# Sums of h from f32 blocks kept at the norm, and seven-product pairs in place of the plain gates

## Chip, cores and metric

The kernel runs on one NeuronCore of a Trainium2 chip. The metric is the device time of one execution in microseconds; the median of the runs counts. The engines are TensorE (PE: matmuls and transposes), VectorE (DVE), ScalarE (ACT), GpSimd (POOL) and SyncE (SP), which issues the DMAs.

## The reference

A decoder trunk of two layers over 1024 tokens of width 1024, in float32. What matters here is the first half of a layer:

```python
for l in range(DEPTH):
    h = rmsnorm(x, norm1[l])
    proj = h @ w_in[l]                       # 1024 x 5120
    qa, ka, va, qb, kb, vb, gate_pre = jnp.split(proj, splits, axis=-1)
    o_a = dilated_mixture(...)               # 12 heads in 3 groups, softmax with ALiBi
    o_b = stick_breaking_attention(...)      # 4 heads
    gates = jax.nn.sigmoid(gate_pre + b_gate[l])    # 2 x 1024 columns
    merged = g_a * (o_a @ w_br[l, :OUT_A]) + g_b * (o_b @ w_br[l, OUT_A:])
    x = x + merged @ w_o[l]
    ...                                      # RMSNorm, gated ConvFFN, residual
```

## The kernel before, in words

**Numbers in two parts.** Each float32 operand of a matmul is kept as a high part in the fp32r format and a low part (the rest). `split` (L133 on) makes them: a copy on ScalarE (L139) gives `hi`, a subtraction on VectorE (L146) gives `lo`. One product takes three matmuls: hi x hi, lo x hi, hi x lo.

**Two ways to multiply by h.** h lies transposed in SBUF: `H[n]` has its high and low parts for token half n, eight blocks k of 128 features by 512 tokens. A *plain* product (`product`, L174 on) adds eight blocks, 8 x 3 = 24 matmuls of 512 columns, for 128 columns of weights and one token half. A *pair* (`pair`, L1053 on) takes two such chunks of weights as one 2 x 2 block matrix and h as another (token half by feature half) and multiplies them by a scheme of seven block products in place of eight. `seven` (L979 on) does one of them, 4 x 3 = 12 matmuls, so a pair has 84 matmuls where two plain chunks have 96. Each pair makes its sums of weights (two on GpSimd at L1075 and L1076, two on VectorE), splits seven pieces of weights (`piece`, into buffers of the tags `wh` and `wl`, four each), and adds partial results on VectorE (`u` tiles). A pair's steps before its first product are seven stages of a generator; `READY` is 6 of them.

**The sums of h.** The scheme also needs four combinations of h's blocks, which are the same for every pair: `S[1]` to `S[4]`, each four tiles of 128 x 512 in two parts. With b11 = h(1,0), b12 = h(0,0), b21 = h(1,1), b22 = h(0,1), where h(n,k) is token half n, feature half k: S1 = b12 - b11, S3 = b22 - b12, S2 = b22 - S1, S4 = b21 - S2 (up to the naming of the blocks). A pair's products take, in this order, h(1,0), S1, S2, h(0,1), S3, h(1,1), S4. `block_sums` (L989 on) makes them from the parts of h, each block being hi + lo: `first` takes three instructions on GpSimd for one quarter of S3 and of S1 (L999, L1004, L1005), `second` two on VectorE (L1012, L1013) for S2, `fourth` three on VectorE (L1019 to L1021) for S4; `in_two` splits them.

**The order.** TensorE's instructions run in the order in which the program emits them. The other engines are ordered by a list scheduler that goes by priority, that is by the place of emission, by readiness and by explicit dependences (`add_manual_dep`, NO_SYNC for order alone). A layer begins with the *head* (`head`, L593 on): values, keys and queries of the first two stick-breaking heads as plain products, beside the norm that still makes h (`first` in layer 0, which normalises eight token blocks as x arrives; `norm`, L513, in layer 1). Then `attend` runs the items of attention: 16 rows of stick-breaking (B), 4 near heads (N), 16 far items (T). Between their small matmuls it calls `dense.advance(rate)`, which emits *units* of six dense matmuls, so many per call as the rate says (`RATE`, `RATE_N`, `RATE_T`). `Dense.choose` (L224) says which: while `plain` has gates, these; then `main`: the near pair 2, `EARLY` gate pairs, and the pairs of values, keys and queries that later items need; and then the other gate pairs (`seven`). The side steps of `block_sums` are emitted one at a time by `aside`, in the head and between units.

**The plain gates.** `gate` (L1207 on) makes one chunk of 128 gate columns for both halves by plain products. The first `PLAIN` = 4 of the 16 chunks of a layer go this way, right behind the head, while the sums of h are made; the other 12 are six pairs (`pair_gate`).

**Buffers** are shared by tag: `e8` (six of 8 KB a partition: the head's weights, the parts of S1 to S3), `xa` (four: x, keys and values of the attention, `stay` rows), `ql` (two: values of the head, raw weights `in_a` of a pair), `p4` (four), `wr` (two: raw weights, `u`), `pt` (six small ones). A tile waits until a buffer of its tag is free.

Of the kernel before, what the change touches and what calls it, by code (L numbers as in the profile page):

```python
# [45 lines left out]
RATE_T = 0.6  # L46
PLAIN = 4
EARLY = 3
# [14 lines left out]
def trunk_kernel(ctx, tc, x, norm1, w_in, b_gate, w_br, w_o, norm2, w_up, conv_w, conv_b, w_down, norm_f, out, depth=None, probe=None):  # L63
# [156 lines left out]
    class Dense:  # L220
# [278 lines left out]

    def new_s(t):  # L500
# [12 lines left out]
    def norm(n, gain, tag, then=None, keep=False):  # L513
# [16 lines left out]
        new_h(n)  # L530
        for e in range(KD):
            hf = kept_f32(n, e) if keep else small("hf")
# [13 lines left out]
    def values_part(vt, w, ms):  # L546
        for m in ms:
# [17 lines left out]
            if m % 2:  # L565
                nc.sync.dma_start(sv[0][:, :, 2 * m - 2 : 2 * m + 2, :], f32(vt[m // 2]))
# [26 lines left out]
    def head(l):  # L593
# [18 lines left out]
        for n in range(2):  # L612
            yield from kq_half(0, wk, n)
            yield from kq_half(1, wq, n)
            if n == 0 and not l:
                yield from values_part(vt, wv, range(2, 4))
        if l:
            yield from values_part(vt, wv, range(2, 4))
# [370 lines left out]
    def block_sums(dense):  # L989


        last, rs = {}, {}

        def first(t, a, b, i):
            if i == 0:
                new_s(t)
                rs[t] = quarter("h_sum") if t == 3 else sb.tile([P, 4, HF], F32, tag="ql", bufs=2, name="h_sum")
            r, (ah, al), (bh, bl) = rs[t][:, i, :], a()[i], b()[i]
            one = pool.tensor_tensor(r, f32(al), f32(bl), ALU.subtract)  # L999
            if last:  # L1000
                tc.add_manual_dep(one.ins, last["sum"], NO_SYNC, reason="one sum after the other")
            else:
                tc.add_manual_dep(one.ins, LAST["h"], SYNC, reason="after h")
            pool.tensor_tensor(r, r, f32(ah), ALU.add)  # L1004
            last["sum"] = pool.tensor_tensor(r, r, f32(bh), ALU.subtract).ins.name  # L1005

        def second(i):
            if i == 0:
                new_s(2)
            in_two(1, i)  # L1010
            r, (ah, al) = rs[1][:, i, :], b22()[i]
            dve.tensor_tensor(r, f32(ah), r, ALU.subtract)  # L1012
            dve.tensor_tensor(r, r, f32(al), ALU.add)  # L1013

        def fourth(i):
            if i == 0:
                S[4] = half(0, 0)
            r, (ah, al) = small("h_sum"), b21()[i]
            dve.tensor_tensor(r, f32(ah), f32(S[2][i][0]), ALU.subtract)  # L1019
            dve.tensor_tensor(r, r, f32(S[2][i][1]), ALU.subtract)  # L1020
            dve.tensor_tensor(r, r, f32(al), ALU.add)  # L1021
            split(*S[4][i], r, "waits")

        def in_two(t, i):
            split(*S[t][i], rs[3 if t == 3 else 1][:, i, :], "waits", LAST["head"])

        b11, b12, b21, b22 = (lambda n=n, k=k: half(n, k) for k in range(2) for n in (1, 0))
        todo = []

        def series(after, lag, gap, f, g):  # L1030

            at = {}
            for i in range(4):
                at.setdefault(i * gap, []).append(lambda i=i: f(i))
                at.setdefault(i * gap + lag, []).append(lambda i=i: g(i))
            for k in range(3 * gap + lag + 1):
                todo.append((after, lambda fs=at.get(k, ()): [h() for h in fs]))

        for i in range(4):
            todo.append((set(), lambda i=i: first(3, b22, b12, i)))  # L1040
        for i in range(4):
# [1045 lines left out]
```

## Time and profile before

| | |
|---|---|
| median of 3 runs | 2643.26 us (2642.09 to 2644.81) |
| profiled execution, its own time | 2642.11 us |
| span in the profile, first to last instruction | 2640.1 us |
| matmuls, all forms | 12780 |
| VectorE, ScalarE, GpSimd busy | 2068.6, 1337.7, 734.9 us |
| DMA | 468.25 MB, mean 177 GB/s |

The profile is of one execution. In its rows, L12 is line 12 of the kernel, an operation is written as out<-in by the names of the tiles, with partitions x elements, and x40 is a count. A group's row gives the busy time, the mean duration of one, and the idle time of the engine just before them with what ended it. In a timeline the first number is the start in us from the beginning of the span and the second how long the instruction, or several merged, took; idle time before stands in brackets. An answer on one tile gives the shortest, median and longest duration in ns and the first and last start. A window row gives, for a stretch of time, the busy time and count of PE, weight loads (PEld), DVE, ACT and POOL, the granted clock of TensorE, the share of the DMA engines and GB/s.

Layer 0's head goes up to about 65 us, its plain gates with the first rows of stick-breaking between them from 65.0 to 120 us, and the first pair follows. In layer 1 the head ends at 1370.2 us and the gates at 1424.4 us.

### The profile page before, as it was taken

How to read it: one execution, taken by the hardware profiler on the slowest of the kernel's cores; microseconds unless marked ns; L12 is line 12 of the kernel's file. 1: busy time of each engine (PE TensorE's matmuls, PEld its weight loads, DVE VectorE, ACT ScalarE, POOL GpSimd, SP SyncE). 2: the span in 40 equal slices, each digit the busy share in tenths (PEclk: the TensorE clock that was granted, in tenths of full speed). 3: DMA queues.
4: the chain of work that ended last, by engine and by line, in shares of the span. 5: the costliest groups of instructions: out<-in, count | busy, mean ns of one | idle time of the engine just before them, and what ended most of it. 6: DMA issues, size and time to landing. Idle time of an engine off the chain costs nothing.

```text
span 2640.1 us, 36792 instructions
## 1 busy us (share of the span) xinstructions
PE 2621.5 (99%) x12780; PEld 2192.0 (83%) x12780; DVE 2068.6 (78%) x3094; ACT 1337.7 (51%) x2488; POOL 734.9 (28%) x612
## 2 busy tenths in 40 slices
PE   9999999999999999999999999999999999999999
PEld 8888888888888888888888888888888888888888
DVE  5887766795888898897659787667858888888865
ACT  5555565564545555432435555666645455554225
POOL 5422201132244343321162212101321343334200
PEclk9999999999999999999999999999999999999999
DMA  7343587873244444688442445797632544357863
GB/s 259 114 144 112 159 220 204 220 253 90 81 146 146 164 146 157 234 310 322 155 154 93 145 140 160 198 236 203 219 101 80 168 144 159 136 176 256 330 247 116
DMA packets 400550, 468.25 MB, mean 177 GB/s; under 512 B 24437, under 2 KB 315629, under 8 KB 398573
## 3 DMA queue, kind: packets, MB, share of 16 engines
q1 hardware_dynamic: 400348, 465.90, 54.9%
q8 instruction: 101, 1.65, 0.3%
q14 instruction: 85, 0.69, 0.1%
q10 hardware_dynamic: 16, 0.00, 0.0%
HBM read 303.23 MB, written 162.59 MB: 176 GB/s over the span
## 4 chain that ended last, share of the span: by engine, by line
PE 83%; DVE 9%; issue 3%; DMA 2%; ACT 2%; POOL 1%; SPq 0%; DVEq 0%; POOLq 0%; ACTq 0%
PE u_a L983 5%; PE u_a L985 5%; PE u_a L984 5%; PE d_ps L1715 5%; PE d_ps L1716 5%; PE d_ps L1717 5%; PE i_a L983 4%; PE i_a L985 4%; PE i_a L984 4%; PE u_c L985 3%; PE u_c L983 3%; PE u_c L984 3%; PE o_ps L180 2%; PE o_ps L181 2%; PE o_ps L182 2%
## 5 line engine op out<-in xcount | busy, mean ns | idle before, releaser
L146 DVE TENSOR_TENSOR w_lo<-up_a,w_hi 128x512 fp32r<-128x512 f32 x240 | 236.7, 992 | 20.2 <-ACT w_hi L139 20.2
L139 ACT CAST w_hi<-up_a 128x512 fp32r<-128x512 f32 x240 | 149.4, 623 | 183.9 <-PE u_a L984 45.9
L1723 DVE TENSOR_TENSOR x<-x,d_ps 128x512 f32<-128x512 f32 (+1 forms) x228 | 151.8, 671 | 78.0 <-PE d_ps L1717 76.6
L1454 POOL TENSOR_TENSOR cv<-cv 128x512 f32<-128x512 f32 x88 | 131.8, 1509 | 248.8 <-DVE cv L1449 138.9
L139 ACT CAST w_hi<-in_a 128x512 fp32r<-128x512 f32 x192 | 119.2, 621 | 117.5 <-PE i_c L984 42.7
L146 DVE TENSOR_TENSOR w_lo<-in_a,w_hi 128x512 fp32r<-128x512 f32 x192 | 141.3, 736 | 36.4 <-ACT w_hi L139 27.0
L146 DVE TENSOR_TENSOR g<-cv,g 128x512 fp32r<-128x512 f32 x154 | 151.7, 986 | 5.2 <-ACT g L139 2.8
L1715 PE MATMUL d_ps<-gd_in,w_hi 128*128 128x512 f32 (+1 forms) x340 | 130.3, 383 | 2.3 <-ACT w_hi L139 1.4
L1717 PE MATMUL d_ps<-gd_in,w_lo 128*128 128x512 f32 (+1 forms) x340 | 129.8, 382 | 0.0
L1716 PE MATMUL d_ps<-gd_in,w_hi 128*128 128x512 f32 (+1 forms) x340 | 129.8, 382 | 0.0
L1075 POOL TENSOR_TENSOR u<-in_a 128x512 f32<-128x512 f32 x32 | 45.8, 1431 | 293.2 <-DMA in_a<-in_w_in_dram 110.5
L983 PE MATMUL u_a<-hh,w_hi 128*128 128x512 f32 x320 | 124.7, 390 | 0.4 <-DVE u L1605 0.3
L984 PE MATMUL u_a<-t_lo,w_hi 128*128 128x512 f32 x320 | 124.5, 389 | 0.0
L985 PE MATMUL u_a<-t_hi,w_lo 128*128 128x512 f32 x320 | 124.5, 389 | 0.0
L985 PE MATMUL u_a<-hh,w_lo 128*128 128x512 f32 x320 | 124.5, 389 | 0.0
L983 PE MATMUL u_a<-t_hi,w_hi 128*128 128x512 f32 x320 | 124.5, 389 | 0.0
L984 PE MATMUL u_a<-hl,w_hi 128*128 128x512 f32 x320 | 124.5, 389 | 0.0
L146 DVE TENSOR_TENSOR w_lo<-w_raw,w_hi 128x512 fp32r<-128x512 f32 x96 | 77.5, 809 | 57.6 <-ACT w_hi L139 52.8
L691 POOL TENSOR_SCALAR_AFFINE_SELECT beta<-beta 128x128 f32<-128x128 f32 x64 | 36.6, 571 | 305.2 <-ACT beta L687 305.2
L139 ACT CAST g<-cv 128x512 fp32r<-128x512 f32 x154 | 94.9, 616 | 39.8 <-POOL cv L1454 29.3
L1715 PE MATMUL d_ps<-gd_in,wd 128*128 128x512 f32 (+1 forms) x292 | 113.9, 390 | 0.0
L1717 PE MATMUL d_ps<-gd_in,wd 128*128 128x512 f32 (+1 forms) x292 | 112.8, 386 | 0.0
(395 smaller groups left out, 8638.0 us busy)
## 6 DMA issues: line engine op xcount, KB each, us to landing
gd<-g SPq DMA_DIRECT2D x154, 512.0 KB, 3.1
gd_in<-gd SPq DMA_DIRECT2D x154, 512.0 KB, 6.3
up_a<-in_w_up_dram SPq DMA_DIRECT2D x80, 512.0 KB, 5.6
in_a<-in_w_in_dram SPq DMA_DIRECT2D x64, 512.0 KB, 5.4
wd_raw<-in_w_down_dram SPq DMA_DIRECT2D x22, 1024.0 KB
gin<-gs SPq DMA_DIRECT2D x32, 512.0 KB, 5.1
w_raw<-in_w_o_dram SPq DMA_DIRECT2D x64, 256.0 KB, 2.9
t_kq<-tk SPq DMA_DIRECT2D x32, 384.0 KB, 5.0
```

The lines of the kernel that those rows point to most:

```text
L139: one = act.copy(hi, src)
L146: two = dve.tensor_tensor(lo, src, f32(hi), ALU.subtract)
L180: pe.matmul(o, lh, rh, start=(first and i == 0), stop=False, skip_group_check=share)
L181: pe.matmul(o, lh, rl, start=False, stop=False, skip_group_check=share)
L983: pe.matmul(o, w[0][:, c], rh, start=(first and i == 0), stop=False, skip_group_check=True)
L984: pe.matmul(o, w[0][:, c], rl, start=False, stop=False, skip_group_check=True)
L985: pe.matmul(o, w[1][:, c], rh, start=False, stop=(last and i == 3), skip_group_check=True)
L1454: return lambda: pool.tensor_tensor(dst, a, b, ALU.subtract)
L1715: pe.matmul(o[:, sub], wh[:, c], gh[:, sub], start=(i == 0 and k in (0, 4, 5)), stop=False, skip_group_check=True)
L1716: pe.matmul(o[:, sub], wh[:, c], gl[:, sub], start=False, stop=False, skip_group_check=True)
L1717: pe.matmul(o[:, sub], wl[:, c], gh[:, sub], start=False, stop=(i == m - 1), skip_group_check=True)
L1723: dve.tensor_tensor(x, x, o[:, sub], ALU.add)
```

## The change

1. The norm keeps h in f32. `raw_h` allocates `RAW[n, k]`, four tiles of 128 x 512 for token half n and feature half k, two in `e8` (n = 0) and two in `xa` (n = 1). The norm writes its f32 result there instead of into a small scratch tile before it is split. In layer 0 the first three token blocks are normalised another way, and `again` fills their 384 columns with hi + lo, eight additions on GpSimd.
2. The sums are made from these f32 blocks: `sum3`, `sum1`, `sum2` on VectorE and `sum4` on GpSimd, one instruction for each quarter, some in place. They are emitted as side steps in the head; S1 and S2 are split there too, S3 and S4 in the first units of the first pair (`begin`).
3. `PLAIN` and `gate` go; all 16 gate chunks are eight pairs, five of them early (`EARLY` 3 to 5). The first pair (near pair 2) follows the head at once.
4. `dense.prime(1)` advances the first pair's preparation by a stage, at fixed places of the head: its loads, its sums on GpSimd, and the splits of three pieces. `{"wv"}` holds the first split back until the values' products have freed `wh` and `wl` in layer 0.
5. Dependences for order alone: a pair's loads behind `LAST["sv"]` (the values' store), its first sum and the clearing of the slots behind `again`. The split of S1 and S2 is no longer put behind the head's last evictions.
6. `RATE_T` goes from 0.6 to 0.55.

```diff
-RATE_T = 0.6
-PLAIN = 4
-EARLY = 3
+RATE_T = 0.55
+EARLY = 5
 ...
+        def prime(self, most):
+            if self.nxt is None:
+                self.nxt = self.choose()
+            self.ready(self.nxt, most)
 ...
+    def raw_h(n):
+        for k in range(2):
+            x = quarter("h_raw") if n else big("h_raw").rearrange("p a (b c) -> p (a b) c", c=HF)
+            RAW[n, k] = x
 ...
-            hf = kept_f32(n, e) if keep else small("hf")
+            hf = kept_f32(n, e) if keep else RAW[n, e // 4][:, e % 4, :] if raw else small("hf")
 ...
-                nc.sync.dma_start(sv[0][:, :, 2 * m - 2 : 2 * m + 2, :], f32(vt[m // 2]))
+                LAST["sv"] = nc.sync.dma_start(sv[0][:, :, 2 * m - 2 : 2 * m + 2, :], f32(vt[m // 2])).ins.name
 ...
-            pool.memset(f32(R["slots"][64:128, :, 1, :]), 0.0)
+            one = pool.memset(f32(R["slots"][64:128, :, 1, :]), 0.0)
+            tc.add_manual_dep(one.ins, LAST["again"], NO_SYNC, reason="behind")
 ...
     def block_sums(dense):
 ...
+        b12, b22, b11, b21 = (lambda i, n=n, k=k: RAW[n, k][:, i, :] for n in range(2) for k in range(2))
+        def sum3(i):
 ...
+            one = dve.tensor_tensor(s3[i], b22(i), b12(i), ALU.subtract)
+            tc.add_manual_dep(one.ins, LAST["h"], NO_SYNC, reason="behind h")
+        def sum1(i):
+            dve.tensor_tensor(b12(i), b12(i), b11(i), ALU.subtract)
+        def sum2(i):
+            dve.tensor_tensor(b11(i), b11(i), s3[i], ALU.add)
+        def sum4(i):
+            pool.tensor_tensor(b21(i), b21(i), b11(i), ALU.subtract)
+        def in_two(t, i):
 ...
+            split(*S[t][i], {1: b12, 2: b11, 3: s3.get, 4: b21}[t](i), "waits", LAST["head"] if t > 2 else None)
+        def front(i):
+            sum3(i)
+            sum1(i)
             in_two(1, i)
+            sum2(i)
+        todo = [(set(), lambda i=i: front(i)) for i in range(4)]
+        todo += [(set(), lambda: dense.prime(1)), (set(), lambda: [sum4(i) for i in range(4)])]
+        todo += [({"wv"}, lambda: dense.prime(1))]
+        todo += [(set(), lambda i=i: in_two(2, i)) for i in range(4)]
+        todo += [(set(), lambda: dense.prime(1)) for _ in range(2)]
         def begin():
             for i in range(4):
-                dense.at(1 + 2 * i, lambda i=i: fourth(i))
+                dense.at(1 + i, lambda i=i: in_two(3, i))
+                dense.at(6 + i, lambda i=i: in_two(4, i))
 ...
-        pool.tensor_tensor(u2, a11, a21, ALU.subtract)
+        one = pool.tensor_tensor(u2, a11, a21, ALU.subtract)
+        tc.add_manual_dep(one.ins, LAST["again"], NO_SYNC, reason="behind")
 ...
-        dense.plain = [gate(l, c) for c in range(PLAIN)]
-        gates = [pair_gate(dense, l, e) for e in range(PLAIN // 2, KD)]
+        gates = [pair_gate(dense, l, e) for e in range(KD)]
 ...
-                hf = small("hf").rearrange("p (e t) -> p e t", e=4)
+                hf = RAW[n, h][:, :, c * P : (c + 1) * P]
 ...
+        def again():
+            t = slice(0, 3 * P)
+            for e in range(KD):
+                k = e % 2
+                hi, lo = (f32(y[:, 4 * k + e // 2, t]) for y in H[0])
+                one = pool.tensor_tensor(RAW[0, k][:, e // 2, t], hi, lo, ALU.add)
+                tc.add_manual_dep(one.ins, LAST["h"], NO_SYNC if e else SYNC, reason="after h")
+            LAST["again"] = one.ins.name
```

More of the change, by code (lines that the diff above doesn't have):

```diff
@@ L989, in block_sums @@
     def block_sums(dense):
-        last, rs = {}, {}
-        def first(t, a, b, i):
-            if i == 0:
[L996 to L1005, printed above, removed]
@@ L1024, in in_two @@
[L1024 to L1037, printed above, removed]
@@ L1204, in pair_gate @@
         return pair(dense, l, (OFF_G + e * P, OFF_G + D + e * P), False, put)
-    def gate(l, c):
-        ab, e = c % 2, c // 2
-        cc = ab * KD + e
-        w = weights(w_in[l][:, OFF_G + cc * P : OFF_G + (cc + 1) * P], P)
-        yield
-        for n in range(2):
-            o = bank("ps", "g_ps")
-            yield from product(o, [(w[k], h_part(n, k)) for k in range(KD)])
-            t = small("gt")
-            act.copy(t, o)
-            nc.sync.dma_start(gs[e, n, :, ab, :], t)
-            yield
     def wo_chunk(l, n, e):
```

65 lines of the change are left out of this document (32 added, 33 removed).

## The prediction

> **What bounds the kernel now.** I read the page of the profile first (its totals, its chain, its rows of slices), then the timeline of TensorE around the place of the change, then the windows by stage, and last the answers on the two tiles that the change removes or re-makes, `g_ps` and `h_sum`.
>
> ```profile
> span 2640.1 us, 36792 instructions
> PE 2621.5 (99%) x12780; PEld 2192.0 (83%) x12780; DVE 2068.6 (78%) x3094; ACT 1337.7 (51%) x2488; POOL 734.9 (28%) x612
> PEclk9999999999999999999999999999999999999999
> PE 83%; DVE 9%; issue 3%; DMA 2%; ACT 2%; POOL 1%; SPq 0%; DVEq 0%; POOLq 0%; ACTq 0%
> ```
>
> TensorE is busy 99% of the span at full granted clock, and 83% of the chain that ended last is on it. Busy alone is weak, since neighbouring matmuls overlap in the record, so I take the pace from the starts. Between the first and the second row here lie the 24 matmuls of one product (8 blocks by 3):
>
> ```profile
> 53.40 0.40 PE L180 MATMUL kq_ps<-hh,kq_w 128*128 128x512 f32 x1
> 58.86 0.39 PE L180 MATMUL q_ps<-hh,kq_w 128*128 128x512 f32 x1
> ...
> 65.04 0.50 PE L180 MATMUL g_ps<-hh,w_hi 128*128 128x512 f32 x1
> ...
> 1358.63 0.28 PE L180 MATMUL v_ps<-v_w,hh 128*128 128x256 f32 x1
> ```
>
> (58.86 - 53.40) / 24 = 0.2275 us for a 512-column matmul. That is the price of one on the path; its recorded 0.39 us is not. The third row is where the head of layer 0 ends and the first plain gate begins.
>
> One rule speaks against the full price: the Trainium skill, "Perfetto Trace Analysis", section Identifying the Most-Contended Engine, says that matmul occupancy misjudges how near TensorE is to its limit and that the busy share of weight loads should be taken beside it. Here that share is 83%, and an estimate by that page would let 83% of the removed time come back, 9.1 us of the 10.9 below. The trace doesn't bear it out in this stretch: 24 matmuls start at an even pace.
>
> **What is removed from TensorE.** The plain gates are these three groups:
>
> ```profile
> L180 PE MATMUL g_ps<-hh,w_hi x128: 389/393/498, 65.0 to 1423.7; 128*128 128x512 f32 x128
> L181 PE MATMUL g_ps<-hl,w_hi x128: 387/389/397, 65.4 to 1424.0; 128*128 128x512 f32 x128
> L182 PE MATMUL g_ps<-hh,w_lo x128: 388/389/403, 65.6 to 1424.2; 128*128 128x512 f32 x128
> ```
>
> 3 x 128 = 384 matmuls, 192 in each layer: four chunks, two halves, 24 each. Two chunks as one seven-product pair take 7 x 4 x 3 = 84. Four chunks thus go from 192 to 168, and 24 matmuls leave each layer: 48 x 0.2275 = **10.9 us** gross. The order behind them stays: in units of six matmuls the gates were 32 and the two new pairs are 28, so everything after comes 4 units earlier. `RATE_T` 0.55 for 0.6 takes about the same 4 units out of the far items (16 items, about 5 calls each, 0.05 less per call), so the tail keeps its filling. The gain is cashed in that stage, if TensorE bounds it, which is weighed among the rivals.
>
> **What the gates covered.** Before, the sums of h were made on GpSimd and VectorE under 52 us of plain gates. After, the first pair starts where 65.04 stands. Its seven products are 12 matmuls, 2.7 us, each: the first needs plain h, the second S1 (+2.7 us), the third S2 (+5.5), the fifth S3 (+10.9), the seventh S4 (+16.4). So S1, S2 and three weight pieces must be made in the head. The first two rows here are the last low parts of h in layer 0, of token blocks 6 and 7 of the eight; the others are gate weights that go (4.3 us):
>
> ```profile
> 38.70 0.69 DVE L146 TENSOR_TENSOR hl<-hf,hh 128x512 fp32r<-128x512 f32 x1 [0.17 <-ACT hh L139]
> ...
> 42.49 0.69 DVE L146 TENSOR_TENSOR hl<-hf,hh 128x512 fp32r<-128x512 f32 x1 [0.69 <-ACT hh L139]
> ...
> 52.09 2.44 DVE L146 TENSOR_TENSOR w_lo<-w_raw,w_hi 128x512 fp32r<-128x512 f32 x2 [2.94 <-ACT w_hi L139]
> ...
> 56.61 0.98 DVE L146 TENSOR_TENSOR w_lo<-w_raw,w_hi 128x512 fp32r<-128x512 f32 x1 [1.48 <-ACT w_hi L139]
> 58.41 0.88 DVE L146 TENSOR_TENSOR w_lo<-w_raw,w_hi 128x512 fp32r<-128x512 f32 x1 [0.81 <-ACT w_hi L139]
> ```
>
> The windows show the room: layer 0 from 44 to the end of the head, and layer 1 (1346 to 1370); the second and third rows are the gates' stretch and the first two pairs of before, the last is from the far stage.
>
> ```profile
> 44.00:65.00 21.00, 21.00 (x133) 18.74 (x131) 6.29 (x7) 4.74 (x9) 20.16 (x16) 1.00 0.64 204
> 64.40:117.00 52.60, 51.49 (x249) 42.26 (x249) 43.77 (x60) 28.71 (x55) 26.00 (x25) 1.00 0.37 114
> 117.00:160.00 43.00, 42.22 (x207) 34.26 (x207) 40.68 (x61) 25.99 (x55) 12.11 (x14) 1.00 0.44 137
> 1346.00:1370.00 24.00, 24.00 (x152) 21.82 (x151) 2.76 (x4) 2.37 (x4) 23.00 (x19) 1.00 0.44 140
> 480.00:520.00 40.00, 40.00 (x247) 35.19 (x245) 31.77 (x64) 20.98 (x51) 5.42 (x6) 1.00 0.69 177
> ```
>
> The columns are the length, then busy time of TensorE, weight loads, VectorE, ScalarE and GpSimd. In both heads GpSimd is full and VectorE nearly empty: 6.29 of 21 us and 2.76 of 24. The change turns that around.
>
> **The new work in the heads.** VectorE gets 12 sums (`sum3`, `sum1`, `sum2`, four each), the 8 low parts of S1 and S2, and 4 instructions of the first pair's pieces. The nearest rows:
>
> ```profile
> L146 DVE TENSOR_TENSOR t_lo<-h_sum,t_hi x24: 658/680/1777, 66.2 to 1416.5; 128x512 fp32r<-128x512 f32 x24
> L1004 POOL TENSOR_TENSOR h_sum<-h_sum,hh x16: 1281/1294/1629, 45.6 to 1376.6; 128x512 f32<-128x512 f32 x16
> L1019 DVE TENSOR_TENSOR h_sum<-hh,t_hi x8: 659/678/1777, 120.1 to 1437.3; 128x512 f32<-128x512 f32 x8
> ```
>
> 24 x 0.68 = 16.3 us on VectorE when it is alone. With GpSimd at work one costs up to 1.78: 1.1 more for each meeting, and this timeline shows three in a row at 1.6 each, beside GpSimd instructions of 1.62 instead of 1.29:
>
> ```profile
> 66.21 4.80 DVE L146 TENSOR_TENSOR t_lo<-h_sum,t_hi 128x512 fp32r<-128x512 f32 x3
> ...
> 67.14 1.62 POOL L1004 TENSOR_TENSOR h_sum<-h_sum,hh 128x512 f32<-128x512 f32 x1
> ```
>
> So one meeting per GpSimd instruction. Layer 0 has `again` (8 additions over 384 of 512 columns, 0.97 us each by that share, from 39.4 to 47 or, with meetings, 49: some 4 after 44), the pair's two weight sums and four `sum4`: about 10 meetings, 11 us; layer 1 has 6, 6.6 us. The Trainium skill, "SBUF — State Buffer", section SBUF: two separate sides, has the same as an exclusive lock, held for the whole instruction, with the other side fully blocked. By that rule a meeting costs up to a whole GpSimd instruction, 1.29 us, the two layers' 16 meetings an estimated 20.6 us where the rows give 17.6, and layer 0 ends 1.9 us later. The trace agrees that one of the two waits, with 1.78 against 0.68.
>
> Layer 0: 21 - 6.29 + 4.3 = 19.0 us are free, and S2 may be 5.5 us later: 24.5. Needed: 16.3 to 27.3. That is from 8 us early (nothing to gain: TensorE is full there) to 2.8 late; the rows of meetings are the nearest, so I take **2.0 us** late. Layer 1: 24 - 2.76 + 5.5 = 26.7 free against 16.3 to 22.9: in time; I take **0.3** for w1, which is wanted at once (bounds 0 and 1). ScalarE (8 + 3 casts) has 16 us free and isn't late. The new waits: `u2` and the slots' clearing stand behind `again` on GpSimd, but the slots are read only by the scores, eight units into the first pair, and `u2` first by its fifth product; the pair's two loads stand behind the first values' store on SP, ahead of the second half's k and q stores, and are issued before half of the head is over. Cover gone there would cost one landing, 5.4 us:
>
> ```profile
> in_a<-in_w_in_dram SPq DMA_DIRECT2D x64, 512.0 KB, 5.4
> ```
>
> **VectorE in the first two pairs.** Of the 43.77 us in the gates' stretch these groups go or move (`in_a` rows: the first pair's pieces):
>
> ```profile
> L146 DVE TENSOR_TENSOR t_lo<-h_sum,t_hi 128x512 fp32r<-128x512 f32 x12 | 11.9, 1018 | 0.0
> L146 DVE TENSOR_TENSOR w_lo<-w_raw,w_hi 128x512 fp32r<-128x512 f32 x4 | 5.0, 1258 | 2.2 <-ACT w_hi L139 2.2
> L1012 DVE TENSOR_TENSOR h_sum<-hh,h_sum 128x512 f32<-128x512 f32 x4 | 3.5, 866 | 0.0
> L1013 DVE TENSOR_TENSOR h_sum<-h_sum,hl 128x512 f32<-128x512 f32 x4 | 2.7, 682 | 0.0
> L146 DVE TENSOR_TENSOR w_lo<-in_a,w_hi 128x512 fp32r<-128x512 f32 x2 | 1.3, 674 | 0.0
> L1080 DVE TENSOR_TENSOR in_a<-in_a 128x512 f32<-128x512 f32 x1 | 0.7, 672 | 0.0
> ```
>
> 43.8 - 25.1 = 18.7 us stay. Added: low parts of S3 and S4 (8), two pairs at 7 low parts, 2 weight sums and 3 additions (24, less 4 in the head), 4 for the near pair's k and q, 4 of the third pair: 36 x 0.68 = 24.5. Together 43.2 us in 52.6 - 5.4 = 47.2: 92%. The stretch 117 to 160 shows what such a load costs: VectorE at 95% (40.68 of 43), TensorE idle 0.78. I take **0.8** a layer (bounds 0 and 2). In turn that later stretch loses the 16 instructions of `fourth`, 10.9 us, and with them at most its 0.78; I take **0.3** a layer back.
>
> Sum: -10.9 + 2.0 + 0.3 + 1.6 - 0.6 = -7.6 us. The profiled execution took 2642.1, 1.2 less than the median of the runs, 2643.3, so 2634.5 in its terms and **2635.6 us** as a median. What a measurement here can tell from no change is 0.2%, 5.3 us.
>
> **The rivals.** *The heads run late.* If the meetings cost what they can (2.8 in layer 0), VectorE takes w1 behind S2 (2.7 more in each layer) and the first pairs wait 2 us in each, then -10.9 + 2.8 + 5.4 + 4.0 = +1.3: 2644.6, no difference. For it: `sum1` needs `again`, which ends only about 49. Against: VectorE's emptiness.
>
> *VectorE becomes the bound of the first pairs (slower).* S1 and S2 live in a group of six buffers that the head's weights and the kept blocks fill. If their buffers came free only when the head ends, 12 low parts and pieces would fall behind it: 12 x 0.68 + 6 x 1.1 = 14.8 us, for which 47.2 - 43.2 = 4.0 us are spare. TensorE waits 10.8 in each layer: -10.9 + 21.6 = +10.7, 2654.0 us. It decides from 9.5 us a layer behind the head on (4.0 spare and half of 10.9). Against it: in layer 1 the k and q weights are last read where the row at 1358.63 stands, 11.6 us before the head ends, and each kept block is free once its sum is made.
>
> *The far stage isn't bound by TensorE.* Then four units less of filling bring nothing, and the costs stay: 2.0 + 0.3 + 1.6 - 0.6 = +3.3, 2646.6, no difference either. By the rule from the Trainium skill's "Perfetto Trace Analysis" above, the weight loads' 35.19 of 40 us in that stage would speak for it in part. Against: the last window has TensorE at 40.00 of 40, VectorE at 31.77. That the matmuls don't go at all I rule out: the counts follow from the code.
>
> **How the numbers follow.** Forecast 0.68, heads late 0.12, far stage 0.05, VectorE the bound 0.15. The forecast's own span goes from all costs nil (10.9 and the later stretches' 1.6 gained: 2630.8) to a gain of 5.3 (2638.0); all costs at their bounds (2.8 + 1 + 4, a gain of 3.1) already belong to the late heads. The range 2631 to 2645 takes the late heads in and leaves out the last two, 0.20. Faster 0.68; within 0.2%: 0.12 + 0.05 and nothing else, 0.17; slower 0.15.
>
> **What would show it.** Right: no `g_ps`; 48 matmuls fewer; GpSimd near half empty in the heads, VectorE near full there; the first pair starting at about 64.4 and 1370.2 and lasting, without the attention's work in it, at most 21 us; VectorE over 90% in the two pairs with under 2 us idle on TensorE. Wrong: `i_a` or `i_c` waiting in the first pair for `t_lo` or `w_lo` by 5 us or more in either layer; matmul starts inside the head spread by evictions queued behind sums; waits in the far items that were not there.

## The result, and the profile after

The changed kernel takes 2669.61 us (median of 4 runs, 2669.03 to 2675.12), the kernel before 2643.15 (4 runs beside it). The ratio is 1.0104, 95% interval 1.0087 to 1.0122: 1% slower, where 2635.6 us had been forecast. The profiled execution took 2669.75 us, its span is 2667.6.

The page of the profile after:

```profile
span 2667.6 us, 36682 instructions
PE 2619.4 (98%) x12732; PEld 2190.2 (82%) x12732; DVE 2072.7 (78%) x3110; ACT 1347.4 (51%) x2500; POOL 696.2 (26%) x588
PE 84%; DVE 9%; DMA 3%; ACT 2%; issue 2%; POOL 0%; SPq 0%; DVEq 0%; ACTq 0%; POOLq 0%
```

TensorE has the 48 matmuls fewer (12780 to 12732), and it idles 48.2 us of the span where it idled 18.6 before. The page doesn't say where; the windows by stage do (length, then busy time of TensorE, weight loads, VectorE, ScalarE, GpSimd, then the granted clock):

```profile
44.00:77.20 33.20, 23.93 (x142) 21.05 (x141) 27.25 (x33) 9.61 (x19) 14.71 (x11) 0.85 0.49 162
57.00:67.20 10.20, 3.40 (x8) 2.75 (x9) 10.20 (x14) 4.84 (x9) 3.84 (x3) 0.50 0.21 77
1357.70:1390.70 33.00, 28.66 (x167) 25.17 (x165) 25.80 (x32) 9.44 (x19) 11.12 (x7) 0.95 0.44 140
...
436.00:563.90 127.90, 125.47 (x733) 108.31 (x732) 88.60 (x197) 74.67 (x168) 14.26 (x15) 0.99 0.81 216
1750.80:1877.90 127.10, 124.35 (x733) 106.91 (x732) 87.91 (x197) 74.46 (x168) 15.08 (x15) 1.00 0.79 217
```

At the end of layer 0's head TensorE now works 24 of 33 us, for 142 matmuls where 21 us held 133 before, and for ten of these microseconds the granted clock is 0.50. The rows of TensorE with their waits, in the two heads and where the first pairs start:

```profile
63.80 0.80 PE L179 MATMUL kq_ps<-hh,kq_w 128*128 128x512 f32 x1 [9.27 <-DVE vb L577]
64.40 0.63 PE L180 MATMUL kq_ps<-hl,kq_w 128*128 128x512 f32 x1
64.82 0.63 PE L181 MATMUL kq_ps<-hh,kq_w 128*128 128x512 f32 x1
...
77.17 0.50 PE L999 MATMUL i_a<-hh,w_hi 128*128 128x512 f32 x1
...
1371.50 0.80 PE L179 MATMUL q_ps<-hh,kq_w 128*128 128x512 f32 x1 [4.34 <-DVE kq_l L593]
```

The first pair starts at 77.17; before, the first gate started at 65.04. TensorE stood 9.27 us, and behind it the matmuls start 0.42 us apart (64.40 to 64.82) instead of 0.2275. It waited for `vb`, the eviction of a values product. This is VectorE's queue in that time, with one row of GpSimd put first:

```profile
53.44 1.61 POOL L1026 TENSOR_TENSOR h_raw<-h_raw 128x512 f32<-128x512 f32 x1 [0.69 <-issue]
...
47.19 2.10 DVE L1016 TENSOR_TENSOR h_sum<-h_raw 128x512 f32<-128x512 f32 x2
49.22 2.38 DVE L1020 TENSOR_TENSOR h_raw<-h_raw 128x512 f32<-128x512 f32 x2
51.52 1.78 DVE L1023 TENSOR_TENSOR h_raw<-h_raw,h_sum 128x512 f32<-128x512 f32 x1
53.23 2.36 DVE L145 TENSOR_TENSOR t_lo<-h_raw,t_hi 128x512 fp32r<-128x512 f32 x2
...
60.19 2.36 DVE L145 TENSOR_TENSOR t_lo<-h_raw,t_hi 128x512 fp32r<-128x512 f32 x2
62.47 0.68 DVE L1023 TENSOR_TENSOR h_raw<-h_raw,h_sum 128x512 f32<-128x512 f32 x1
63.07 1.27 DVE L577 TENSOR_TENSOR vb<-v_ps,vb 128x512 fp32r<-128x512 f32 x2
```

`vb` runs at 63.07, twice in a row. A *bank* is one of the two buffers of the tag `ps` in which products collect. Both had been full, the older one since about 48.6 us (the end of its product), and VectorE had twelve sums and four low parts in its queue ahead, from 47.19 on without a gap: 16 instructions in 15.9 us. Most take 1.0 to 1.8 us instead of 0.68, beside work of GpSimd (E2 below takes that away).

Layer 1's head has a shorter form of it; the row of GpSimd comes first, then ScalarE, then VectorE:

```profile
1365.09 1.73 POOL L1080 TENSOR_TENSOR in_a<-in_a 128x512 f32<-128x512 f32 x1
...
1366.86 0.62 ACT L138 CAST w_hi<-in_a 128x512 fp32r<-128x512 f32 x1 [6.48 <-POOL in_a L1080]
1367.38 0.59 ACT L592 ACTIVATE kq_h<-q_ps 128x512 fp32r<-128x512 f32 x1
...
1369.57 1.28 DVE L1023 TENSOR_TENSOR h_raw<-h_raw,h_sum 128x512 f32<-128x512 f32 x2
1370.77 0.68 DVE L593 SCALAR_TENSOR_TENSOR kq_l<-q_ps,kq_h 128x512 fp32r<-128x512 f32 x1
```

ScalarE idles 6.48 us over a weight cast that waits for GpSimd's weight sum, with the cast of q queued behind; then q's low part stands behind sums on VectorE, and TensorE waits the 4.34 us above for it.

The stages, by the starts of TensorE's matmuls (first pair, or first plain gate before the change; first `z<-t_kq`; first `br_ps`; first `v_ps` of layer 1), lengths in us, of the kernels that the argument uses most; the rest ends with the start of the last matmul, and E numbers are the experiments below:

| | head 0 ends | attention 0 / 1 | far stage 0 / 1 | head 1 | rest, both layers |
|---|---|---|---|---|---|
| before | 65.04 | 356.39 / 354.25 | 128.59 / 128.59 | 46.85 | 1554.7 |
| after | 77.17 | 358.86 / 360.02 | 127.87 / 127.17 | 52.91 | 1557.5 |
| E1 evictions first | 71.56 | 357.54 / 360.85 | 127.90 / 130.54 | 51.81 | 1558.3 |
| E2 no GpSimd in heads | 71.34 | 357.25 / 363.34 | 125.25 / 128.16 | 47.13 | 1556.9 |
| E5 both | 65.61 | 358.08 / 360.21 | 125.52 / 131.68 | 46.85 | 1556.4 |
| E12 pair sums moved | 66.12 | 355.13 / 356.52 | 128.92 / 127.23 | 46.85 | 1557.6 |
| E14 rates shifted | 65.84 | 352.85 / 351.65 | 126.31 / 128.04 | 46.85 | 1556.0 |

After against before: heads +12.1 and +6.1, attention up to the far stage +2.5 and +5.8, far stage -0.7 and -1.4 where -5.5 each were forecast, rest +2.8, all of it in layer 1: +27.1, the difference of the spans within 0.4.

The second place, in the attention. GpSimd's row, then VectorE's, then TensorE's:

```profile
252.19 1.77 POOL L1078 TENSOR_TENSOR u<-in_a 128x512 f32<-128x512 f32 x1 [5.89 <-PE v_t L1175]
254.04 1.29 POOL L1080 TENSOR_TENSOR in_a<-in_a 128x512 f32<-128x512 f32 x1
255.28 0.29 POOL L707 TENSOR_SCALAR_AFFINE_SELECT beta<-beta 128x128 f32<-128x128 f32 x1
...
255.86 1.23 DVE L720 TENSOR_TENSOR_SCAN stay<-stay,zero 128x512 f32<-128x512 f32 x1 [3.05 <-POOL stay L707]
258.32 0.68 DVE L1181 TENSOR_TENSOR vv<-v_t,vv 128x512 fp32r<-128x512 f32 x1
...
259.15 0.55 PE L745 MATMUL sb_o<-sbh,kv 128*128 128x256 f32 x1 [2.93 <-DVE vv L1181]
```

The next pair's weight sums sit on GpSimd ahead of a mask; VectorE's scan waits 3.05 us for the mask, an eviction stands behind the scan, TensorE 2.93 us behind that. These instructions are those of before. The pairs now come four steps of dense work earlier against the items, which is the likely reason that they meet otherwise; no run shows that alone.

### The profile page after: what moved, and what is told of

Read it like the earlier page. It is cut to its first block, busy times and chain, and to the rows that moved or that the text cites. A ratio compares the mean times of both kernels' runs of the same rounds, so it can differ in the third digit from the quotient of the medians.

```text
span 2667.6 us, 36682 instructions
## 1 busy us (share of the span) xinstructions
PE 2619.4 (98%) x12732; PEld 2190.2 (82%) x12732; DVE 2072.7 (78%) x3110; ACT 1347.4 (51%) x2500; POOL 696.2 (26%) x588
## 4 chain that ended last, share of the span: by engine, by line
PE 84%; DVE 9%; DMA 3%; ACT 2%; issue 2%; POOL 0%; SPq 0%; DVEq 0%; ACTq 0%; POOLq 0%
PE u_a L999 5%; PE u_a L1000 5%; PE u_a L1001 5%; PE d_ps L1708 5%; PE d_ps L1710 4%; PE d_ps L1709 4%; PE i_a L999 4%; PE i_a L1001 4%; PE i_a L1000 4%; PE u_c L999 3%; PE u_c L1000 3%; PE u_c L1001 3%; PE o_ps L181 2%; PE o_ps L179 2%; PE o_ps L180 2%; PE i_c L999 2%
## 5 line engine op out<-in xcount | busy, mean ns | idle before, releaser
L138 ACT CAST w_hi<-in_a 128x512 fp32r<-128x512 f32 x216 | 134.1, 621 | 185.3 <-PE i_a L1000 71.3
L145 DVE TENSOR_TENSOR w_lo<-in_a,w_hi 128x512 fp32r<-128x512 f32 x216 | 161.4, 748 | 51.7 <-ACT w_hi L138 43.7
L1078 POOL TENSOR_TENSOR u<-in_a 128x512 f32<-128x512 f32 x36 | 52.6, 1460 | 399.9 <-DMA in_a<-in_w_in_dram 118.0
L720 DVE TENSOR_TENSOR_SCAN stay<-stay,zero 128x512 f32<-128x512 f32 (+2 forms) x96 | 97.2, 1020 | 33.2 <-POOL stay L707 33.0
L999 PE MATMUL i_a<-t_hi,w_hi 128*128 128x512 f32 x288 | 119.9, 416 | 0.0
L999 PE MATMUL i_a<-hh,w_hi 128*128 128x512 f32 x288 | 119.2, 414 | 0.0
L1001 PE MATMUL i_a<-t_hi,w_lo 128*128 128x512 f32 x288 | 114.5, 398 | 0.0
```

What stands on the lines that cost most here:

```text
L138: one = act.copy(hi, src)
L145: two = dve.tensor_tensor(lo, src, f32(hi), ALU.subtract)
L720: one = dve.tensor_tensor_scan(rev, rev, zero[:, 0:1].to_broadcast([P, c1 - c0]), 1.0 if c1 == L else sv[:, c1 : c1 + 1], ALU.mult, ALU.add)
L999: pe.matmul(o, w[0][:, c], rh, start=(first and i == 0), stop=False, skip_group_check=True)
L1001: pe.matmul(o, w[1][:, c], rh, start=False, stop=(last and i == 3), skip_group_check=True)
```

## The experiments

The theory after the result: in the heads, the sums stand ahead of the evictions in the in-order queues, so the two banks fill and TensorE stops (order). The rival: VectorE, slowed by meetings with GpSimd, has too much to do in the head in any order (load). For the attention: masks behind the pairs' sums on GpSimd.

**E1, evictions first.**

```diff
-            one = act.copy(vv[:, :, :, 0:64], ov)
-            two = dve.tensor_tensor(vv[:, :, :, 64:128], ...)
+            with tc.high_priority(offset=AHEAD):
+                one = act.copy(vv[:, :, :, 0:64], ov)
+                two = dve.tensor_tensor(vv[:, :, :, 64:128], ...)
...
-        LAST["head"] = in_parts(c, SCALE, hi, lo, o)
+        with tc.high_priority(offset=AHEAD):
+            LAST["head"] = in_parts(c, SCALE, hi, lo, o)
```

> The changed kernel with the evictions of the head (values, k, q) given priority over the sums on VectorE and ScalarE; the same work on every engine. Order theory (the evictions stand behind the sums in the queues, TensorE finds both banks full): the wait of 9.4 us at 54 us falls to 2 to 5 us, and the half clock behind it goes with it, so layer 0's first pair starts near 70 instead of 77.2 us, layer 1 gains about 3 more, and the time is 2655 to 2662 us. Load theory (VectorE, slowed by its meetings with GpSimd, cannot do the head's work in time whatever its order): the wait only moves behind the head, into the first products of the first pair, which then wait for t_lo, and the time stays at 2666 to 2672 us.

Measured: 2666.66 us (one execution, as in all experiments for which no interval is given; so the lengths of the stages tell more than the time). The time is on the load theory's side, the place on the other: the head of layer 0 ends 5.6 us earlier, and nothing reappears in the first pair. Rows of VectorE, then TensorE:

```profile
51.87 3.48 DVE L145 TENSOR_TENSOR t_lo<-h_raw,t_hi 128x512 fp32r<-128x512 f32 x2
55.27 0.68 DVE L578 TENSOR_TENSOR vb<-v_ps,vb 128x512 fp32r<-128x512 f32 x1
...
56.00 0.50 PE L179 MATMUL kq_ps<-hh,kq_w 128*128 128x512 f32 x1 [1.75 <-DVE vb L578]
63.61 0.50 PE L179 MATMUL q_ps<-hh,kq_w 128*128 128x512 f32 x1 [1.85 <-DVE vb L578]
```

One wait of 9.27 became 1.75 and 1.85; what is left is a shorter queue ahead of each eviction, whose low parts take 1.74 us each here (3.48 for two). Layer 1's head gains only 1.1, and its attention and far stage lose 4.2.

**E2, no GpSimd in the heads.**

```diff
-            pool.tensor_tensor(b21(i), b21(i), b11(i), ALU.subtract)
+            dve.tensor_tensor(b21(i), b21(i), b11(i), ALU.subtract)
...
-        todo += [(set(), lambda: dense.prime(1)), (set(), lambda: [sum4(i) for i in range(4)])]
+        todo += [(set(), lambda: dense.prime(1)), (set(), lambda: None)]
...
-                dense.at(6 + i, lambda i=i: in_two(4, i))
+                dense.at(6 + i, lambda i=i: [sum4(i), in_two(4, i)])
...
-        one = pool.tensor_tensor(u2, a11, a21, ALU.subtract)
...
-        pool.tensor_tensor(a21, a21, a22, ALU.add)
+        eng = pool if dense.started else dve
+        one = eng.tensor_tensor(u2, a11, a21, ALU.subtract)
...
+        eng.tensor_tensor(a21, a21, a22, ALU.add)
```

> The changed kernel with GpSimd nearly out of the heads: the four sums for S4 are made on VectorE in the pair, just ahead of their splits, and the first pair's two weight sums on VectorE; of GpSimd's work only the rebuilding of h (8 additions) is left in layer 0's head and nothing in layer 1's. VectorE gets 1.4 us more in each head and loses six meetings of 0.6 to 1.1 us. Load theory: six meetings fewer shorten the stretch in which the evictions wait by about 5 us in layer 0, and layer 1's wait of 4.5 us goes; the time is 2655 to 2661 us. Order theory: the queue ahead of the evictions stays as long in instructions, each nearer 0.68 than 1.2 us; the wait at 54 us falls to 5 to 7 us, and the time is 2660 to 2666 us.

Measured: 2657.04 us. The low parts are back at 0.64 us each, and the eviction still waits behind them (VectorE's rows, then TensorE's):

```profile
49.99 1.28 DVE L145 TENSOR_TENSOR t_lo<-h_raw,t_hi 128x512 fp32r<-128x512 f32 x2
...
57.22 0.68 DVE L577 TENSOR_TENSOR vb<-v_ps,vb 128x512 fp32r<-128x512 f32 x1
...
57.96 0.50 PE L179 MATMUL kq_ps<-hh,kq_w 128*128 128x512 f32 x1 [4.43 <-DVE vb L577]
```

Layer 0's wait halves (4.43 us), layer 1's is gone, and its head is 5.8 us shorter. Meetings and order each hold about half in layer 0; in layer 1 it is GpSimd.

**E3, the later pairs' weight sums on VectorE.**

```diff
-        one = pool.tensor_tensor(u2, a11, a21, ALU.subtract)
...
-        pool.tensor_tensor(a21, a21, a22, ALU.add)
+        eng = dve if dense.started else pool
+        one = eng.tensor_tensor(u2, a11, a21, ALU.subtract)
...
+        eng.tensor_tensor(a21, a21, a22, ALU.add)
```

> The changed kernel with the two weight sums of every pair after the first made on VectorE instead of GpSimd. If the waits of 3.1 us at 256 and 1570 us and of 1.9 to 2.1 us at 1410 and 1607 us come from masks (the affine selects) queued behind these sums on GpSimd, with VectorE's scan and an eviction behind it, they go, with the half clock that follows: 8 to 11 us less, 2658 to 2662 us. If they come from VectorE's load, 42 more instructions of 0.68 us a layer there make them worse: 2670 to 2685 us.

Measured: 2673.31 us. Both are true, in different stages: the attention up to the far stage is 4.7 and 4.2 us shorter than in the changed kernel (354.17 and 355.86), the far stage 4.6 and 9.0 longer, where p1's low part is now late:

```profile
445.50 0.39 PE L916 MATMUL o<-p1l,slots 128*128 128x256 f32 x1 [3.17 <-DVE p1l L145]
...
1790.30 0.58 PE L916 MATMUL o<-p1l,slots 128*128 128x256 f32 x1 [3.98 <-DVE p1l L145]
```

**E4, `RATE_T` 0.6 again.**

```diff
-RATE_T = 0.55
+RATE_T = 0.6
```

> The changed kernel with RATE_T 0.6 again, as before. If the far stage is bound by TensorE, the earlier use of the same filling leaves the last far items bare, and the time is 2 to 4 us longer, 2672 to 2674 us; if the far items are bound by their loads and masks' turns, it is the same within 2 us, or shorter by up to 3.

Measured: 2671.49 us, 1.9 above, within what single executions of one kernel differ here (E12). Nothing follows.

**E5, E1 and E2 together.**

> The two edits together: evictions of the head first, and GpSimd out of the heads but for the rebuilding of h. Both at once, because each alone left about half of the wait in layer 0's head. If queue order and meetings are the two factors of one wait (so many sums ahead of the eviction, times the length of each), together they leave 1 to 3 us of the 9.4 us wait at 54 us and no half clock in layer 0's head, so its first pair starts at 66 to 68 us and the time is 2650 to 2654 us. If VectorE simply had too much to do in layer 0's head, the wait moves into the first pair, as t_lo, and the time is that of the run without GpSimd, 2655 to 2659 us.

Measured: 2652.09 us. The windows show the end of layer 0's head:

```profile
44.00:65.60 21.60, 21.60 (x138) 19.32 (x136) 21.55 (x33) 8.28 (x15) 5.33 (x5) 1.00 0.55 190
```

VectorE is busy 21.55 of 21.60 us and TensorE 21.60: the same sums and low parts do fit beside the head, filled to the brim, if evictions pass them and GpSimd stays away. Both heads are back to 65.61 and 46.85. (The sums for S4 are made later here, in the first pair.) So the load theory falls as stated, and so does order alone: the wait was a queue's length times the length of each instruction in it.

**E6 and E12, the pair sums on VectorE until the far stage** (on E5).

```diff
-        eng = pool if dense.started else dve
+        eng = pool if dense.far else dve
...
         for i, (name, first, rest, rate, make) in enumerate(items):
+            dense.far |= name[0] == "T"
```

> The kernel of the run e5_prio_nopool, with the weight sums of the later pairs on VectorE too, but only until the far stage begins, where they stay on GpSimd. All of them on VectorE took 4.7 and 4.2 us of waits out of the stage before the far items and put 4.6 and 9.0 us into the far stage. If the first is the masks' queue on GpSimd and the second VectorE's load, this kernel keeps the first alone: 6 to 9 us below e5_prio_nopool, 2642 to 2647 us. If instead the two stages hang together through the order of the items (a wait avoided early comes back as a wait for t_kq or p1l later), it is within 3 us of e5_prio_nopool.

Measured: 2640.93 us in one execution. The attention up to the far stage is 3.1 and 4.3 us shorter than in E5. In place of the mask's 3.05 us VectorE makes the sums and waits 0.19:

```profile
241.59 0.69 DVE L1082 TENSOR_TENSOR u<-in_a 128x512 f32<-128x512 f32 x1
242.31 0.69 DVE L1083 TENSOR_TENSOR in_a<-in_a 128x512 f32<-128x512 f32 x1
243.19 1.22 DVE L723 TENSOR_TENSOR_SCAN stay<-stay,zero 128x512 f32<-128x512 f32 x1 [0.19 <-POOL stay L710]
```

> The kernel of e6_dve_sticks again, timed in five rounds. One look gave 2640.9 us beside 2643.2 us of the kernel before: 0.9 to 2.3 us faster, a ratio of 0.9991 to 0.9997. If the look was luck, the ratio's interval holds 1.

Measured: 2643.5 us (11 runs, 2638.39 to 2646.76), ratio 1.0002 (0.9993 to 1.0011). That one execution had been a low one. With all known waits of the heads and most of the masks' taken out, the kernel equals the one before, with 48 matmuls fewer: where did their 10.9 us go? They left the far stage, as forecast (733 matmuls instead of 757), and it hardly got shorter: by 1.0 us for both layers in the profiled execution, where head 0 is 1.1 longer, the attention up to the far stage 1.0 and the rest 2.9.

**E7, the gates' part alone, on the kernel before.**

```diff
-PLAIN = 4
-EARLY = 3
-RATE_T = 0.6
+PLAIN = 0
+EARLY = 5
+RATE_T = 0.55
```

> The kernel before with the gates' part of the change alone: no plain gates, five early pairs, RATE_T 0.55, and the sums of h made as before, after the head. What the plain gates covered is then bare: the 8 sums on GpSimd for S1 alone are 8 x 1.29 = 10 us, S2 follows on VectorE, so TensorE stands some 15 to 25 us in each layer's first pair: 2662 to 2690 us. If it comes out under 2655 us, the sums needed less cover than the plain gates gave, and the changed kernel's early sums were not needed.

Measured: 2711.34 us, dearer than expected. The first pair starts 5.5 us late and then waits again for low parts of the sums:

```profile
70.51 0.80 PE L983 MATMUL i_a<-hh,w_hi 128*128 128x512 f32 x1 [5.28 <-DVE kq_l L582]
79.67 0.80 PE L984 MATMUL i_c<-t_lo,w_hi 128*128 128x512 f32 x1 [3.96 <-DVE t_lo L146]
```

The plain gates did cover the sums; sums in the head cost less than bare ones, 26 us instead of 68.

**E8, E9, E10, the far stage's filling** (each one of these edits on E6, in this order).

```diff
-LEAD_T = 3
+LEAD_T = 4
...
-RATE_T = 0.55
+RATE_T = 0.6
...
-RATE_T = 0.55
+RATE_T = 0.5
```

> The kernel of e6_dve_sticks with a far item begun four steps of dense work behind the issue of its loads instead of three. There the far stages still stand 2.7 and 5.1 us over the kernel before in waits, 0.9 and 1.4 us of it where scores wait for the loads of k and q (t_kq). If these loads are late because less dense work lies between issue and use, one step more (1.4 us) takes those waits out: 1 to 3 us less, 2638 to 2640 us. If the loads wait for their buffer or queue, the item is only later: 0 to 3 us more, 2641 to 2644 us.

> The kernel of e6_dve_sticks with RATE_T 0.6, the value before. If 0.55 is right for four steps less of dense work, 0.6 uses the work up before the last items, which then show bare waits for p1l: 1 to 3 us more, 2642 to 2644 us. If the waits in the far stage come from too little dense work between a load's issue and its use, it is 1 to 3 us less, 2638 to 2640 us.

> The kernel of e6_dve_sticks with RATE_T 0.5: less dense work for each far item and more left for the end. If the far stage is short of dense work at its end, it is 0 to 2 us less, 2639 to 2641 us; if the loads' waits decide, these grow by 2 to 4 us, 2643 to 2645 us, with the excess in the early far items.

Measured: 2641.36, 2643.76 and 2647.58 us, one execution each; only the last is beyond E12's spread. By place they tell more. In E8 no wait of TensorE in the far stages is over 0.43 us, and these are together the shortest of all runs, 125.35 and 126.53 us: one step more of dense work between issue and use took the waits for `t_kq` out but for that one. Its time isn't below E6's, since the rest took 1.7 us more there and the stages ahead 0.9. The waits of E9 and E10 differ in kind. E9 (0.6), near the end of the far stage:

```profile
542.68 0.38 PE L919 MATMUL o<-p1l,slots 128*128 128x256 f32 x1 [1.52 <-DVE p1l L145]
```

Dense work is used up 3.2 and 3.8 us before the far stages end (0.23 in E6), and the last items stand bare. E10 (0.5), among the first far items of layer 1:

```profile
1768.75 0.45 PE L639 MATMUL z<-t_kq 128*128 128x128 f32 x1 [5.10 <-DMA t_kq<-tk]
```

Here too little dense work lies between the issue of a load and its use. With 24 matmuls fewer and loads issued three steps ahead, some wait stayed at each of the three rates.

**E11, the first pair's weight sums alone on VectorE.**

```diff
-        one = pool.tensor_tensor(u2, a11, a21, ALU.subtract)
...
-        pool.tensor_tensor(a21, a21, a22, ALU.add)
+        eng = pool if dense.started else dve
+        one = eng.tensor_tensor(u2, a11, a21, ALU.subtract)
...
+        eng.tensor_tensor(a21, a21, a22, ALU.add)
```

> The changed kernel with one edit: the first pair's two weight sums on VectorE. If layer 1's wait of 4.5 us for kq_l comes from these sums on GpSimd (a cast of ScalarE waits for them, and the cast of q stands behind it), it goes with this edit alone, and layer 1's head loses 4 to 6 us; layer 0's wait falls only by the two meetings, 1 to 2.5 us of 9.4: 2660 to 2665 us. If the four sums for S4 are what slows both heads, layer 1's wait stays above 3 us and the time is 2666 to 2670 us.

Measured: 2671.61 us. By place, layer 0's wait fell to 7.70 us and layer 1's to 2.18, half of it: the other half goes in E2, where the sums for S4 leave GpSimd too. The gain of both places didn't show in the time, since layer 1's far stage is 3.5 us longer here.

**E13 and E14, the four steps taken elsewhere** (on E12).

```diff
-RATE_T = 0.55
+RATE_T = 0.6
...
-RATE_N = 0.75
+RATE_N = 0.675
```

That is E13. E14 has the first of the two edits and instead of the second:

```diff
-RATE = (1.1, 1.25, 1.35, 1.4)
+RATE = (1.07, 1.215, 1.315, 1.365)
```

> The kernel of e12_final with RATE_T 0.6 as before and the four steps of dense work (5.5 us) taken from the near items instead, whose rate is 0.675 for 0.75 (53 calls x 0.075 = 4 steps). If the removed matmuls gave nothing because the far stage needs its filling (its loads and p1l are late without it), the far stages come back to 128.6 us with about 2 us of excess, as before, and the near items end 5.5 us earlier in each layer: 2634 to 2639 us. If the items before are as bare without theirs, their waits grow by as much, and the time stays at 2641 to 2646 us.

> The same with the four steps taken from the 16 items of the first attention form instead: RATE 1.07, 1.215, 1.315, 1.365 for 1.1, 1.25, 1.35, 1.4 (116 calls, 4 steps), RATE_N 0.75, RATE_T 0.6. If the far stage alone lacks its filling: 2634 to 2639 us. If the scans and masks of these items set their pace already (9 to 11 us of excess in that stage), their waits grow by 2 to 5 us a layer and the time is 2641 to 2648 us.

Measured: E13 2646.81 us, ratio 1.0015 (1.0005 to 1.0024); E14 **2634.17 us** (2632.69 to 2635.03), ratio **0.9964** (0.9951 to 0.9977), 0.4% faster than the kernel before. Its windows of layer 0's stages from the first pair on:

```profile
65.80:418.70 352.90, 349.34 (x1801) 291.56 (x1801) 274.11 (x492) 203.46 (x436) 31.18 (x65) 1.00 0.53 155
418.70:545.00 126.30, 125.92 (x746) 109.27 (x744) 92.94 (x203) 75.36 (x171) 14.54 (x15) 1.00 0.83 221
```

By starts of matmuls, E14's far stage has 12 of its 24 back (348 dense ones; 360 before the change, 336 in E12) and TensorE is busy 125.92 of 126.30 us in it; the stage before has 12 fewer and is 3.5 us shorter than before the change. In both layers the two stages are together 9.0 us shorter than before, so most of the 10.9 us is there.

E13 missed its 2634 to 2639 us, and its edit didn't do what was expected of it: of the four steps only one, 6 dense matmuls, came back to the far stage (342), with 15 small ones of the items. At the rate of 0.6 the dense work is used up 6.9 and 6.0 us before the stage ends (1.0 in E14), and the last items stand bare, so that the far stages take 131.32 and 130.41 us:

```profile
553.43 0.66 PE L973 MATMUL j_ps<-ident,fx 128*128 128x128 f32 x4 [2.05 <-DVE ot L655]
```

So the far stage did need its filling at that rate, and the first items could spare it. That the near items could not isn't shown, since they gave up so little.

**E15, E14's retuning on the kernel before** (pair sums on VectorE until the far stage, the lower `RATE`).

```diff
-        pool.tensor_tensor(u2, a11, a21, ALU.subtract)
-        pool.tensor_tensor(a21, a21, a22, ALU.add)
+        eng = pool if dense.far else dve
+        eng.tensor_tensor(u2, a11, a21, ALU.subtract)
+        eng.tensor_tensor(a21, a21, a22, ALU.add)
...
-RATE = (1.1, 1.25, 1.35, 1.4)
+RATE = (1.07, 1.215, 1.315, 1.365)
```

> The kernel before with the two edits of e14_less_sticks that it can take: the pairs' weight sums on VectorE until the far stage, and the lower RATE of the first items. If the 9 us that e14_less_sticks gains come from the 48 matmuls fewer, this kernel, which has them all, gains at most the masks' waits of before (1 to 3 us) and may lose as much by the new rates: 2640 to 2645 us. If they come from the retuning and not from the matmuls, it comes out near e14_less_sticks, 2633 to 2637 us.

Measured: 2662.39 us, ratio 1.0073 (1.0057 to 1.009). The attention up to the far stage is 7.3 and 8.6 us longer than before (363.69 and 362.83). The far stages are longer too (131.61 and 131.36), and the time lies beyond both expected ranges. These two edits are no gain in themselves. That the kernel before has no better rates of its own isn't shown.

## Why the prediction was wrong

**The count held, its price was not paid back.** 48 matmuls went, all from the far stage (757 to 733 in each layer's window).

The forecast by stages was -7.6 us and the measured sum is +27.1. The 34.7 us between them are 15.9 in the heads, 8.8 in the far stages, 7.2 in the attention before them and 2.8 in the rest.

**The step that failed is "needed against free" in layer 0's head.** The prediction set 16.3 to 27.3 us of VectorE work against 24.5 free, and took 2.0 us late. The work was sized well. The groups of VectorE from 44 to 77 us:

```profile
L145 DVE TENSOR_TENSOR t_lo<-h_raw,t_hi 128x512 fp32r<-128x512 f32 x8 | 7.2, 949 | 0.0
L1016 DVE TENSOR_TENSOR h_sum<-h_raw 128x512 f32<-128x512 f32 x4 | 4.4, 1150 | 0.0
L1023 DVE TENSOR_TENSOR h_raw<-h_raw,h_sum 128x512 f32<-128x512 f32 x4 | 3.8, 952 | 0.0
L1020 DVE TENSOR_TENSOR h_raw<-h_raw 128x512 f32<-128x512 f32 x4 | 3.7, 954 | 0.0
L145 DVE TENSOR_TENSOR w_lo<-in_a,w_hi 128x512 fp32r<-128x512 f32 x4 | 2.8, 707 | 0.1
```

With 1.4 for two weight additions that is 23.3 us. But the step checked the sums against the pair that reads them, not the evictions that came to stand behind them. The latter have the nearer deadline: two banks, 5.5 to 5.8 us each to fill. The text had it, as a thing that would show it wrong ("evictions queued behind sums"), and gave it no price; its price was 12.1 us in layer 0 (9.3 of wait, 1.6 for 8 matmuls at half clock, the rest in smaller waits) against 2.0. That VectorE would be near full there and GpSimd half empty held roughly (27.25 and 14.71 of 33.20 us), and told nothing of this. The rival *the heads run late* had the place, but priced it by the pair's readers too: 2.8 us for layer 0's sums, and 2644.6 us with all of its costs.

**Layer 1's 0.3 was 6.1** (4.3 of wait, most of the rest half clock behind it). The prediction named who would wait for the first pair's weights, not what was queued behind the waiting cast on ScalarE.

**The far stage.** "The gain is cashed in that stage" held for the matmuls, not for the time: -0.7 and -1.4 us. The rival *the far stage isn't bound by TensorE*, at 0.05, was the nearer one, though its window before had TensorE full: full with filling, which also covered loads and the last items (E9, E10, E13). The size of that error is clearest in E12, whose heads are nearly clean: 1.0 us of 10.9 came back in its far stages. In E8, with loads issued a step earlier, 5.3 did; why not all, with no wait left over 0.43 us, stays open.

**The attention up to the far stage** had no term beyond the first two pairs and the stretch behind them, +0.5 us a layer in all. It lost 2.5 and 5.8 us, for the most part where masks fell behind pair sums (E3, E6). That pairs which come four steps earlier would shift every meeting there was not weighed.

**The forecast for the first two pairs** (0.8 us each layer) was about right in layer 0: from 77.2 to 100 us TensorE is busy 22.06 of 22.80 us, and it idles 0.74 up to 124.2. In layer 1 it idles 1.74 from 1390.75 to 1438. VectorE was 87% busy in both stretches, not over 90%.

```profile
77.20:100.00 22.80, 22.06 (x101) 17.69 (x101) 19.20 (x31) 18.24 (x36) 5.07 (x8) 1.00 0.42 131
```

The slower rival's mechanism, S1 and S2 falling behind the head for want of buffers, did not come: they were made in the head, at TensorE's cost.

Open: the rest, with no term and +2.8 us, all in layer 1. In it lies a wait of 1.74 us for `u` early in the feed-forward part, which stood behind a late load of weights; most descendants of the change have it, at 1.2 to 2.0 us, E13 and the kernel before don't. Nothing was tried on it.

## What to carry to other kernels

Work moved under a stretch where TensorE is full must be checked against the evictions of that stretch, instruction by instruction in the queue: the deadline is a bank's filling time, not the reader of the moved work. Filling taken out of a stage whose loads it covers gave next to nothing here (1.0 of 10.9 us in E12) until the schedule was moved with it (E14), so a few matmuls saved are cashed only where nothing else is late. And one execution is not enough to tell 3 us where a kernel's own executions lie 8 us apart.

## What the runs showed of the hardware

A short wait of TensorE can cost more than itself. In the window 57.00:67.20 above the granted clock is 0.50; before the change the clock was full from 6.2 us to the last matmul. This one began 2.7 us after the start of the last matmul at 54.26 and lasted 10.24 us; others lasted 3.41 or 6.83. Waits of about 2 us could be enough, this one in the changed kernel's far stage:

```profile
476.19 0.30 PE L636 MATMUL z<-t_kq 128*128 128x128 f32 x1 [1.65 <-DMA t_kq<-tk]
```

It was 2.05 us from start to start and was followed by 3.41 us at half clock from 476.8. The Trainium skill, "TensorE: Matmul & The Clock Gate", section HAM oscillation — how this bites in real kernels, warns of idle gaps over about 3.4 us; here shorter ones could do it, and the measurement decides. The length of 3.41 us agrees with the window of 3413 ns that the same page gives in its Part 1.

Not every such wait did it: in the same execution 2.92 us before 1573.61 were followed by no half clock, and 1.90 us before 1609.27 were. The traces show what told them apart. In one execution all half-clock stretches begin on one grid of 3.413 us: those of the changed kernel, at 56.98, 258.36, 476.82, 1371.11 and 1610.04, lie 59, 64, 262 and 70 periods apart. The wait of 1.90 us lay inside one period, which ended at 1610.04 with 1.90 us idle; that of 2.92 was cut by a grid line at 1572.5, with 1.81 us idle on one side and 1.11 on the other. Over all kept traces with such stretches, from 10 us on, every period at full clock with 1.9 us or more of idle TensorE was followed by half clock at once (37 of 37), of those with 1.4 to 1.9 us 11 of 49, of those with less none. What decides between 1.4 and 1.9 stays open.
